# A hybrid decoder step on one core: state-space constants made during the matmul groups on another engine, thirteen groups for eleven, and another order of the output projection's first group

## The chip, the core and the metric

The kernel runs on one core of a Trainium2 chip. The metric is device time in microseconds (us), the median of several runs. "PE" is the matmul engine and "PEld" its weight loads, "DVE" the vector engine, "ACT" the activation engine, "POOL" GpSimd, and "SP" the queue from which most transfers are issued.

## The reference

One layer on 536 tokens (16 meta, 512 prompt, 8 sample) of width 2048 is computed in float32. Attention and an S5 state-space branch run side by side and are merged.

```
h = rmsnorm(x) @ w_in                         # 2048 x 8704: q, k, v, z_a, u, z_s, g_a, g_s
o = sink_attention(rope(q), rope(k), v)       # window 128, meta tokens, sinks
dt = exp(log_dt); lam_bar = exp(lam * dt)     # 64 groups x 64 states, complex
b_bar = (lam_bar - 1) / lam * b
hs = scan(lam_bar, b_bar u) (+ lam_bar^n h0 for the sample group)
y = gelu(Re(c hs) + d u); y = y * sigmoid(y @ w_glu + b_glu)
out = x + (sigmoid(g_a) * ((o * silu(z_a)) @ w_attn_out)
         + sigmoid(g_s) * ((y * silu(z_s)) @ w_ssm_out)) @ w_out
```

## The kernel before

**Matmuls.** Every float32 operand is split into a rounded part and its rest (`xh`, `xl` for x; `whi`, `wlo` for a weight unit of 128 x 1024), and a product is three matmuls: hi by hi, lo by hi, hi by lo. The tokens lie in two halves c of 268 columns, of which a matmul streams 260. A *block* (`mm`, L1002) is one set of 128 output columns: 16 slices kt x 3 x 2 halves = 96 matmuls. For a weight unit, SP loads `raw`, ACT rounds `whi`, and DVE subtracts for `wlo` (L881 to L883).

**Groups.** Some blocks are taken in pairs as a *group* (`quad`): the 2 x 2 of (even or odd kt) x (half) is multiplied in the seven-product way of Strassen and Winograd, on sums of x that `taus` made (`tt`) and on sums of weight units that DVE makes in place (L940). One product is 8 x 3 = 24 matmuls (L1205), a group 168. Of x itself a group reads three of four quarters, `xs[0..2]`: the quarter (even kt, c = 1) is not read by any group. `keep3` (L1217) copies a bank of products to a `z` tile, so that the bank is free for the next group. The two `z` tiles of a group go to `gD` in DRAM at its end (L1039) and are the next group's two `z` tiles.

**Order.** (1) x is loaded and split while three blocks run; (2) six more blocks; (3) eleven groups, q = 0 to 10 (`NQ`); (4) `ORDER1`, 23 blocks: "x" (gates), "h" (heads: k, v, q), "u" (state-space inputs); (5) 13 x blocks and block 47; (6) 8 blocks of the gated unit; (7) 16 of the state-space output; (8) 16 of the attention output (L1511 and on, which also make the sums `cb` of the merged activations); (9) the output projection, eight groups, the first with `late=True`: products 1 to 3 run their first seven of eight slices, then their eighth, when the last `cb` is there, then the others.

**Planner.** `Background` holds generators in lanes. After each half of a weight unit (24 matmuls) `step(budget)` adds a credit, and generators run until their yielded costs have used it; `yield None` waits for the next step. `ssm_prep` (the constants `lam`, `lamp`, `Fk`, `T6`, `T11`, `car` of the state space, some 190 small DVE instructions of 32 to 704 columns) is added at the start of (4) and drained at the first "u". From then on `ssm_sets` and one `ssm(n)` for each "u" run, and at (5) `attention` is added, which begins when they are done. In attention, PE's scores (L656) read `QT`, which DVE makes (L640) from rows loaded from DRAM (`sw`, `sb`, `rb`).

Of the kernel before, what the change touches and what calls it, by code (L numbers as in the profile page):

```python
# [29 lines left out]
def acc_exp(nc, pool, out, x, n):  # L30

    v = nc.vector
# [20 lines left out]
def cmul(nc, pool, out, a, br, bi, sh, tag):  # L53

    v = nc.vector
    n = int(np.prod(sh))
    pat = {1: "p (r a) -> p r a", 2: "p (r a b) -> p r a b"}[len(sh)]
    kw = dict(zip("ab", sh))
    t1 = pool.tile([P, 2 * n], F32, name=tag + "1").rearrange(pat, r=2, **kw)
    t2 = pool.tile([P, 2 * n], F32, name=tag + "2").rearrange(pat, r=2, **kw)  # L60
    v.tensor_tensor(out=t1, in0=a, in1=bc(br, 1, 2), op=ALU.mult)
    v.tensor_tensor(out=t2, in0=a, in1=bc(bi, 1, 2), op=ALU.mult)
    v.tensor_tensor(out=out[:, 0], in0=t1[:, 0], in1=t2[:, 1], op=ALU.subtract)
    v.tensor_tensor(out=out[:, 1], in0=t1[:, 1], in1=t2[:, 0], op=ALU.add)


def ssm_prep(nc, cst, tmp, psum, dram, R, ident, a_prm, a_h0):

    v = nc.vector
    prm = cst.tile([P, 3, 32], F32, name="prm")  # L70
    nc.sync.dma_start(out=prm, in_=a_prm)
    h0 = tmp.tile([P, 32, 2, 8], F32, name="h0")
    nc.sync.dma_start(out=h0, in_=a_h0)
    are, aim, ldt = prm[:, 0], prm[:, 1], prm[:, 2]
    dt = tmp.tile([P, 32], F32, name="dt")
    acc_exp(nc, tmp, dt, ldt, 32)
# [4 lines left out]
    acc_exp(nc, tmp, rho, x, 32)  # L81
# [34 lines left out]
    lam = cst.tile([P, 2, 32], F32, name="lam")  # L116
    v.tensor_tensor(out=lam, in0=e1, in1=bc(rho, 1, 2), op=ALU.mult)
    R["lam"] = lam
# [14 lines left out]
    cmul(nc, tmp, Fq, g, are, naim, (32,), "c32_")  # L133

    lamp = cst.tile([P, 2, 4, 32], F32, name="lamp")
    v.tensor_copy(out=lamp[:, :, 0], in_=lam)
    for k, (a, b) in enumerate(((lam, 0), (lamp[:, :, 1], 0), (lamp[:, :, 1], 1))):
        cmul(nc, tmp, lamp[:, :, k + 1], a, lamp[:, 0, b], lamp[:, 1, b], (32,), "c32_")
    R["lamp"] = lamp
    Fk = cst.tile([P, 8, 32], F32, name="Fk")  # L140
    fv = Fk.rearrange("p (r k) a -> p r k a", r=2)
    v.tensor_tensor(out=fv[:, :, 0], in0=Fq, in1=bc(m2, 1, 2), op=ALU.mult)
    cmul(nc, tmp, fv[:, :, 1:4], bc(fv[:, :, 0], 2, 3), lamp[:, 0, 0:3], lamp[:, 1, 0:3], (3, 32), "c96_")
    nF = cst.tile([P, 2, 32], F32, name="nF")
# [30 lines left out]
    def powers(tab, z, cnt, tag):  # L175
# [4 lines left out]
        for i in range(3):  # L180
            nz = tmp.tile([P, 2, 32], F32, name=f"{tag}z{i}")
            cmul(nc, tmp, nz, zs[-1], zs[-1][:, 0], zs[-1][:, 1], (32,), "c32_")
            zs.append(nz)
        n = 1
        for zp in zs:
# [3 lines left out]
            cmul(nc, tmp, tab[:, :, :, n:n + m], tab[:, :, :, 0:m],  # L189
# [14 lines left out]
    cmul(nc, tmp, Z, zs[2], zs[1][:, 0], zs[1][:, 1], (32,), "c32_")  # L204
# [25 lines left out]
    yield 2.0  # L230
# [579 lines left out]
BUDGET = 5.8  # L810
BUDGET2, BUDGET3, BUDGET4 = 5.2, 2.8, 4.2
# [52 lines left out]
class Stream:  # L864
# [6 lines left out]
    def tiles(self, i, pool=None):  # L871
        raw = self.pool.tile([P, 8, P], F32, name="raw", bufs=3)
# [27 lines left out]
class Quads:  # L900
# [9 lines left out]
    def __init__(self, tc, nc, w, first, n, pool, more_raw, more_parts):  # L910
        self.tc, self.nc, self.w, self.first, self.n, self.pool = tc, nc, w, first, n, pool
        self.more, self.mr, self.mp = None, more_raw, more_parts
# [43 lines left out]
def trunk(tc, A, O):  # L956
# [31 lines left out]
    xh = xp.tile([P, 16, 2, CH], F32R, name="xh")  # L988
    xl = xp.tile([P, 16, 2, CH], F32R, name="xl")
# [21 lines left out]
    def mm_x(w0, **kw):  # L1011
        return mm(2, lambda k, c: xh[:, k, c, w0:CH], lambda k, c: xl[:, k, c, w0:CH], w0, **kw)
# [29 lines left out]
    with tc.tile_pool(name="xld", bufs=2, side="right") as xld:  # L1042
# [25 lines left out]
        for kt in range(16):  # L1068
# [9 lines left out]
            nc.scalar.activation(out=xh[:, kt], in_=xr, func=AF.Copy, scale=gain[:, kt:kt + 1])  # L1078
# [3 lines left out]
            v.scalar_tensor_tensor(out=xl[:, kt], in0=xr, scalar=gain[:, kt:kt + 1], in1=xh[:, kt].bitcast(F32),  # L1082
                                   op0=ALU.mult, op1=ALU.subtract)
            for (_, wh, wl), ps in zip(w3, ps3):
                for (wt, xo, f, l) in ((wh, xh, kt == 0, False), (wh, xl, False, False), (wl, xh, False, kt == 15)):
                    for c in range(2):
                        nc.tensor.matmul(ps[:, c, 0:260], lhsT=wt[:, kt % 8], rhs=xo[:, kt, c, 8:CH], start=f, stop=l)  # L1087
# [35 lines left out]
    S, sp, Ds = {}, None, {}  # L1123
# [85 lines left out]
    def quad(qs, x, banks, y, done, late=False, step=lambda: None):  # L1209
# [10 lines left out]
        W = [qs.get() for n in range(4)] if late else None  # L1220
        for n, (bank, k) in enumerate(first):
            if n == 3 and W:
                for m in range(3):
                    product(first[m][0], W[m], x[first[m][1]], False, range(7, 8))
                    keep3(m)
            product(bank, W[n] if W else qs.get(), x[k], n < 3, range(7) if n < 3 and W else range(8))
            if n in (0, 2) and not W:
# [9 lines left out]
        product(a, qs.get(), x[1], True)  # L1237
# [59 lines left out]
    def xpart(k, c):  # L1297
        return lambda p, e: (xh, xl)[e][:, 2 * p + k, c, 8:CH]

    xs = [xpart(0, 0), xpart(1, 0), xpart(1, 1)] + [lambda p, e, n=n: tt[p][:, e, n] for n in range(4)]  # L1300
    for q in range(NQ):
        y = [ev.tile([P, 2, 260], F32, name="z") for n in range(2)]
# [5 lines left out]
        def step():  # L1308
            nonlocal nst
            nst += 1  # L1310
            if q == NQ - 1:
# [13 lines left out]

    scst = tc.tile_pool(name="scst", bufs=1, side="right")
    sc = scst.__enter__()
    spp = tc.tile_pool(name="spp", bufs=1, side="right")
    bg.add(ssm_prep(nc, sc, spp.__enter__(), aux, dram, S, C["idn"], A["prm"], A["h0"]))
    for n_, (kind, n) in enumerate(ORDER1):  # L1330
        if kind == "x":
            xblock(**({} if n_ else dict(pool=aux, name="aux")))
# [7 lines left out]
        if sp is None:  # L1340
            bg.drain()
            spp.__exit__(None, None, None)
# [10 lines left out]
            for t in (S["H"][:, :, :, 8], *(d[:, :, 0] for d in S["d0"])):  # L1353
                nc.gpsimd.memset(t, 0.0)
            S["bu"] = [aux.tile([P, 512], F32, name=n) for n in ("tr", "wg")] + [S["ax"][:, 0]]
            S["kp"] = S["ax"][:, 1, 0:P]
# [344 lines left out]
```

## Time and profile before

| | |
|---|---|
| median of 3 runs | 1285.49 us (1284.97 to 1285.79) |
| the profiled execution | 1285.47 us, span 1283.7 us |
| mean granted clock of PE | 0.996 |
| PE, DVE, ACT, POOL busy | 99%, 75%, 47%, 9% of the span |

A matmul's record is longer than its turn, since matmuls overlap. So a busy PE only says that PE never stood; the turn of one matmul is read from stretches without a gap, length by count.

### The profile page before, as it was taken

To read this page: it belongs to the slowest core of one execution; us is meant where nothing else is said; L and a number is where in the kernel's file an instruction comes from. 1 tells how busy PE (TensorE), PEld (TensorE's weight loads), DVE (VectorE), ACT (ScalarE), POOL (GpSimd) and SP (SyncE) were. 2 spreads that over 40 slices of the span, in tenths; PEclk is the share of its full clock that TensorE was granted. 3 is DMA by queue.
4 is the path that set the end of the run, shared out by engine and by line. 5 is a ranking of instruction groups with operands and counts; after the bars stand their busy time and mean duration, and the time that the engine had idled before them with its cause. 6 is when DMAs were issued, how large, how long until landed. Compare 5 with 4: busy or idle time off the path is not lost.

```text
span 1283.7 us, 26443 instructions
## 1 busy us (share of the span) xinstructions
PE 1266.4 (99%) x10453; PEld 1240.4 (97%) x10453; DVE 963.6 (75%) x1689; ACT 608.7 (47%) x1300; POOL 114.4 (9%) x231
## 2 busy tenths in 40 slices
PE   9999999999999999999999998999999999999998
PEld 8999999999999999999999998999999999999998
DVE  8586788777697567887778649889986567887775
ACT  8554354444426755445522233486556533344342
POOL 0000000000001222222252021111100000000000
PEclk9999999999999999999999998999999999999999
DMA  8544344333435555554553479767765456545441
GB/s 281 209 156 160 117 141 128 125 120 108 142 115 187 171 149 142 160 149 145 161 129 112 135 223 296 237 203 226 255 229 170 147 181 192 186 150 159 144 143 51
DMA packets 102832, 212.86 MB, mean 166 GB/s; under 512 B 21580, under 2 KB 41988, under 8 KB 102676
## 3 DMA queue, kind: packets, MB, share of 16 engines
q1 hardware_dynamic: 94260, 193.77, 47.3%
q0 software_dynamic: 8448, 17.40, 5.3%
q8 instruction: 82, 1.34, 0.4%
q14 instruction: 42, 0.34, 0.1%
HBM read 178.91 MB, written 33.13 MB: 165 GB/s over the span
## 4 chain that ended last, share of the span: by engine, by line
PE 91%; DMA 5%; ACT 2%; DVE 1%; SPq 1%; issue 0%; ACTq 0%; DVEq 0%
PE mm L1002 53%; PE pr L1205 26%; PE wg L705 2%; DMA gD<-z 1%; PE aux L1205 1%; DMA sw<-rawD 1%; PE aux L1002 1%; PE mm L1087 1%; DMA raw<-in_w 1%; PE aux L656 1%; PE aux L657 1%; PE mm L1456 1%; DMA xr<-in_x 1%; PE wg L436 1%; PE tr L436 1%; ACT whi L941 1%
## 5 line engine op out<-in xcount | busy, mean ns | idle before, releaser
L1002 PE MATMUL mm<-xh,whi 128*128 128x260 f32 (+1 forms) x1312 | 270.7, 288 | 0.0
L1002 PE MATMUL mm<-xl,whi 128*128 128x260 f32 (+1 forms) x1312 | 268.7, 285 | 0.0
L1002 PE MATMUL mm<-xh,wlo 128*128 128x260 f32 (+1 forms) x1312 | 268.0, 285 | 0.0
L882 ACT CAST whi<-raw 128x1024 fp32r<-128x1024 f32 (+3 forms) x144 | 139.2, 975 | 223.7 <-PE mm L1002 104.6
L1002 PEld LDWEIGHTS mm<-xh,whi 128*128 128x128 f32 x1312 | 204.2, 190 | 2.9 <-issue 1.6
L942 DVE TENSOR_TENSOR wlo<-raw,whi 128x1024 fp32r<-128x1024 f32 x133 | 159.8, 1223 | 62.7 <-ACT whi L941 58.6
L1002 PEld LDWEIGHTS mm<-xl,whi 128*128 128x128 f32 x1312 | 205.1, 189 | 1.2 <-issue 1.2
L1002 PEld LDWEIGHTS mm<-xh,wlo 128*128 128x128 f32 x1312 | 203.3, 189 | 1.9 <-issue 1.9
L883 DVE TENSOR_TENSOR wlo<-raw,whi 128x1024 fp32r<-128x1024 f32 (+3 forms) x144 | 162.1, 1131 | 52.6 <-ACT whi L882 50.6
L941 ACT CAST whi<-raw 128x1024 fp32r<-128x1024 f32 x133 | 137.2, 1048 | 133.7 <-PE pr L1205 51.9
L1205 PE MATMUL pr<-cb,whi 128*128 128x260 f32 x848 | 153.4, 283 | 2.7 <-ACT whi L941 2.7
L1205 PEld LDWEIGHTS pr<-cb,whi 128*128 128x128 f32 x848 | 130.9, 189 | 3.3 <-ACT whi L941 3.3
L1002 PE MATMUL mm<-Y,whi 128*128 128x260 f32 x768 | 131.3, 289 | 0.0
L1205 PE MATMUL pr<-tau,whi 128*128 128x260 f32 x672 | 121.2, 283 | 0.0
L1205 PE MATMUL pr<-cb,wlo 128*128 128x260 f32 x424 | 119.0, 283 | 0.0
L1002 PEld LDWEIGHTS mm<-Y,whi 128*128 128x128 f32 x768 | 107.4, 189 | 5.0 <-issue 4.2
L1205 PEld LDWEIGHTS pr<-tau,whi 128*128 128x128 f32 x672 | 103.1, 188 | 0.0
L940 DVE TENSOR_TENSOR raw<-raw 128x1024 f32<-128x1024 f32 x76 | 92.9, 1222 | 1.5
L1205 PE MATMUL pr<-tau,wlo 128*128 128x260 f32 x336 | 93.7, 283 | 0.0
L1002 PE MATMUL mm<-A,whi 128*128 128x260 f32 x512 | 82.1, 283 | 0.0
L1002 PE MATMUL mm<-Y,wlo 128*128 128x260 f32 x384 | 79.8, 287 | 0.0
L1205 PEld LDWEIGHTS pr<-cb,wlo 128*128 128x128 f32 x424 | 79.6, 188 | 0.0
(427 smaller groups left out, 2273.2 us busy)
## 6 DMA issues: line engine op xcount, KB each, us to landing
raw<-in_w SPq DMA_DIRECT2D x202, 512.0 KB, 4.3
gD<-z SPq DMA_DIRECT2D x48, 260.0 KB, 2.8
t<-gD SPq DMA_DIRECT2D x32, 260.0 KB, 2.6
cache<-in_vc POOLq DMA_DIRECT2D x16, 286.0 KB, 4.4
cache<-in_kc POOLq DMA_DIRECT2D x15, 288.0 KB, 5.9
xr<-in_x SPq DMA_DIRECT2D x16, 268.0 KB, 4.8
xg<-in_x SPq DMA_DIRECT2D x8, 536.0 KB, 4.3
sD<-z SPq DMA_DIRECT2D x16, 260.0 KB, 2.3
```

The lines of the kernel that those rows point to most:

```text
L436: nc.tensor.matmul(o[n], lhsT=D["CL"][:, 2 * e + n, i, 1:5], rhs=H[:, 2 * e + n, i, 0:140], start=False, stop=(i == 1))
L656: nc.tensor.matmul(ps[:, e, 0:272], lhsT=q, rhs=KH[:, k0:k0 + 272], start=True, stop=False)
L657: nc.tensor.matmul(ps[:, e, 0:272], lhsT=q, rhs=KL[:, k0:k0 + 272], start=False, stop=True)
L705: nc.tensor.matmul(pv[64 * e:64 * e + 64, 0:256], lhsT=V, rhs=pr[:, e::2], start=(i == 0), stop=(i == len(parts) - 1))
L882: nc.scalar.copy(out=hi, in_=raw)
L883: self.dve = nc.vector.tensor_tensor(out=lo, in0=raw, in1=hi.bitcast(F32), op=ALU.subtract).ins
L940: nc.vector.tensor_tensor(out=o, in0=o, in1=i, op=ALU.add)
L941: nc.scalar.copy(out=hi, in_=t)
L942: nc.vector.tensor_tensor(out=lo, in0=t, in1=hi.bitcast(F32), op=ALU.subtract)
L1002: m = nc.tensor.matmul(ps[:, c, 0:W], lhsT=wt[:, k], rhs=xo(kt, c), start=f, stop=l)
L1087: nc.tensor.matmul(ps[:, c, 0:260], lhsT=wt[:, kt % 8], rhs=xo[:, kt, c, 8:CH], start=f, stop=l)
L1205: m = nc.tensor.matmul(bank, lhsT=wt[:, p], rhs=x(p, e), start=first and f and p == 0, stop=l and p == 7, skip_group_check=not first and l ...
```

## The change

- `NQ` is 13, and `ORDER1` has one "x" instead of three and another order; with that 11 instead of 13 x blocks are left for (5).
- x is stored as three quarters (`xh`, `xl`, 8 x 3 x 268) and a fourth in tiles of its own (`xhq`, `xlq`). After the first blocks the fourth's tiles become work space `flats`. In the last group `again` writes the constants from there to DRAM, loads the quarter's x anew (8 transfers) and splits it again; the constants are read back at the start of (4).
- `ssm_prep` runs in the groups with a credit of 0.4 a product. Its `tensor_tensor`, `tensor_scalar`, `tensor_copy` and `memset` go to POOL, the rest (8 `scalar_tensor_tensor` and a `reciprocal`) stays on DVE. What depends on the sample's state is a generator of its own (`ssm_states`), run from the first "u".
- A group's two output tiles are `z` for even q and `t` for odd q while `nx < 31` (q to 10), and `z` afterwards.
- In the output projection's first group the product with `x[1]` is fourth; the first four products run seven slices each, then the eighth slices. Its weights come from the fourth `raw`, which has a place of its own (`fourth`) and is loaded during the last block of (8).

```diff
+class Mostly:
+    def __init__(self, a, b):
+        self.a, self.b = a, b
+    def __getattr__(self, name):
+        return getattr(self.a if name in ("tensor_tensor", "tensor_scalar", "tensor_copy", "memset") else self.b, name)
...
-def ssm_prep(nc, cst, tmp, psum, dram, R, ident, a_prm, a_h0):
-    v = nc.vector
+def ssm_prep(nc, K, tmp, psum, dram, R, ident, a_prm, later):
+    v = Mostly(nc.gpsimd, nc.vector)
...
+def ssm_states(nc, cst, pool, R, a_h0):
+    v = nc.vector
+    A0, N0 = (cst.tile([P, 32, 2, 8], F32, name=n) for n in ("A0", "N0"))
+    nc.sync.dma_start(out=A0, in_=a_h0)
...
+GBUDGET = 0.4
-NA, NQ = 4, 11
+NA, NQ = 4, 13
-ORDER1 = [(k, 0) for k in "xxxhhuhhuhuhhuhuhhuhuhu"]
+ORDER1 = [(k, 0) for k in "xuhuhuhhuhhuhhuhhuhhu"]
...
+            if k == 3 and self.fourth:
+                pool, bufs = self.fourth, 1
...
+        if r < 7 and self.fourth:
+            s = (0, 1, 2, 5, 3, 4, 6)[s]
...
-    xh = xp.tile([P, 16, 2, CH], F32R, name="xh")
-    xl = xp.tile([P, 16, 2, CH], F32R, name="xl")
+    xh, xl = (xp.tile([P, 8, 3, CH], F32R, name=n) for n in ("xh", "xl"))
+    quarter = {}
+    def quarters():
+        for t, n in ((xh, "xhq"), (xl, "xlq")):
+            quarter[id(t)] = xp.tile([P, 8, CH], F32R, name=n)
+    def xk(t, kt, c, w0):
+        if (kt % 2, c) == (0, 1):
+            return quarter[id(t)][:, kt // 2, w0:CH]
+        return t[:, kt // 2, (0, 1 + c)[kt % 2], w0:CH]
+    def xkeep(kt, src, c):
+        g = gain[:, kt:kt + 1]
...
+        for (h, l), s in zip(dst, src):
+            nc.scalar.activation(out=h, in_=s, func=AF.Copy, scale=g)
+        yield
+        for (h, l), s in zip(dst, src):
+            v.scalar_tensor_tensor(out=l, in0=s, scalar=g, in1=h.bitcast(F32), op0=ALU.mult, op1=ALU.subtract)
+        yield
...
-        W = [qs.get() for n in range(4)] if late else None
+        W = [qs.get() for n in range(4)] if late else []
+        early = [(first[n][0], W[n], x[first[n][1]]) for n in range(3)] + [(a, W[3], x[1])] if late else []
+        for p in early:
+            product(*p, True, range(7))
+        for n, p in enumerate(early):
+            product(*p, False, range(7, 8))
+            if n < 3:
+                keep3(n)
...
+    flats = [xp.tile([P, 8 * CH], F32, name="work", tag=n) for n in ("xhq", "xlq")]
+    bg.add(ssm_prep(nc, kept(flats[0][:, 0:NKEPT]), Places([flats[1], flats[0][:, NKEPT:]], spots()), aux, dram, S, C["idn"],
+                    A["prm"], lambda: tc.issue_after(bg.last)))
+    kD = dram.tile([P, NKEPT], F32, name="kept")
+    def again():
+        nc.sync.dma_start(out=kD, in_=flats[0][:, 0:NKEPT])
+        quarters()
+        raw = [qs.more.tile([P, 8, P], F32, name="raw", bufs=3).rearrange("p k n -> p (k n)") for _ in range(3)]
+        raw = [raw[n // 3][:, CH * (n % 3):CH * (n % 3) + CH] for n in range(8)]
+        for n, r in enumerate(raw):
+            nc.sync.dma_start(out=r, in_=A["x"][:, 2 * n, 1])
+        yield 0.0
+        yield None
+        for n, r in enumerate(raw):
+            list(xkeep(2 * n, r, 1))
+            yield 0.5
     for q in range(NQ):
-        y = [ev.tile([P, 2, 260], F32, name="z") for n in range(2)]
+        if q == NQ - 1:
+            bg.drain()
+        y = [ev.tile([P, 2, 260], F32, name="zt"[q % 2 * (nx < 31)]) for n in range(2)]
...
+            if (q, nst) == (NQ - 1, 3):
+                bg.add(again())
+            bg.step(GBUDGET if q < NQ - 1 else 1.2)
...
-    bg.add(ssm_prep(nc, sc, spp.__enter__(), aux, dram, S, C["idn"], A["prm"], A["h0"]))
+    kt_ = sc.tile([P, NKEPT], F32, name="kept")
+    nc.sync.dma_start(out=kt_, in_=kD)
...
-            bg.drain()
-            spp.__exit__(None, None, None)
...
+            bg.add(ssm_states(nc, sc, sp, S, A["h0"]), lane=1)
             bg.add(ssm_sets(), lane=1)
...
+    qs.fourth = ent(tc.tile_pool(name="fourth", bufs=1))
...
-            qs.load(i - 12)
+            qs.load(i - 11)
```

## Rows read from the trace of the kernel before

**Rows 1.** The page: busy time of each engine with its share of the span and its instructions, and the clock granted to PE in 40 slices (tenths of full speed).

```profile
PE 1266.4 (99%) x10453; PEld 1240.4 (97%) x10453; DVE 963.6 (75%) x1689; ACT 608.7 (47%) x1300; POOL 114.4 (9%) x231
PEclk9999999999999999999999998999999999999999
```

**Rows 2.** The chain that ended last, in order of time (start us, us, what): a long piece of the blocks, one of the groups; a transfer at the start of attention; pieces of the output projection's first group.

```profile
56.67 58.64 PE mm L1002 x486
...
139.28 94.04 PE pr L1205 x783
...
774.55 9.77 DMA sw<-rawD
...
1113.96 2.52 PE aux L1205 x21
1116.49 5.05 PE pr L1205 x42
...
1121.86 1.05 ACT whi L941
...
1130.09 0.94 ACT whi L941
```

**Rows 3.** Busy time by stretch (us from the span's start, then PE, PEld, DVE, ACT, POOL with instructions, granted clock, DMA share, GB/s): the first of eleven stretches that cover the groups and the sum over the eleven; the stretch after the groups; two at the start of attention.

```profile
115.30:135.50 20.20, 20.20 (x171) 20.20 (x170) 17.30 (x17) 9.89 (x14) 0.00 (x0) 1.00 0.35 118
...
sum 222.70, PE 220.23 PEld 219.40 DVE 168.54 ACT 102.37 POOL 0.00; mean PE 20.02 PEld 19.95 DVE 15.32 ACT 9.31 POOL 0.00
...
338.00:396.50 58.50, 58.50 (x484) 58.50 (x483) 50.13 (x220) 15.78 (x20) 0.00 (x0) 1.00 0.40 126
...
787.50:789.60 2.10, 0.00 (x0) 0.00 (x0) 2.07 (x4) 1.56 (x3) 0.55 (x1) 1.00 1.00 357
789.70:796.40 6.70, 6.08 (x28) 6.08 (x29) 6.64 (x11) 2.27 (x4) 0.54 (x1) 0.50 0.97 287
```

**Rows 4.** Waits, who for whom: us in total, times, longest us. The first three are of the groups (115 to 340 us), the fourth of the start of attention (738 to 805 us), the last of the output projection's beginning (1100 to 1150 us).

```profile
ACT whi L941 <- PE pr L1205: 40.9, 24, 4.1
ACT z L1217 <- DMA gD<-z: 37.7, 17, 3.2
...
PE pr L1205 <- ACT z L1217: 2.4, 3, 1.3
...
PE aux L656 <- DVE QT L640: 4.3, 1, 4.3
...
PE pr L1205 <- ACT whi L941: 2.7, 3, 1.3
```

**Rows 5.** DVE in the groups (115 to 338 us) by line: count | busy us, mean ns | idle before. `wlo`, the sums of weights, an output's scaling, and an addition of half that width.

```profile
L942 DVE TENSOR_TENSOR wlo<-raw,whi 128x1024 fp32r<-128x1024 f32 x75 | 90.2, 1223 | 37.4 <-ACT whi L941 36.8
L940 DVE TENSOR_TENSOR raw<-raw 128x1024 f32<-128x1024 f32 x42 | 51.4, 1223 | 0.9
L1032 DVE TENSOR_TENSOR z<-z,R 128x520 f32<-128x520 f32 x20 | 13.9, 697 | 0.4
...
L1239 DVE TENSOR_TENSOR z<-z,pr 128x260 f32<-128x260 f32 x11 | 4.6, 419 | 0.0
```

**Rows 6.** Single lines (min/median/max ns, first and last start us, forms): POOL's only instruction that reads SBUF; two of the constants' instructions on DVE; `wlo` and `keep3` over the whole kernel.

```profile
L651 POOL COPY S<-k_attc x16: 188/232/739, 755.5 to 989.8; 128x4 f32<-128x4 f32 x16
...
L47 DVE TENSOR_TENSOR ex_q<-ex_q,ex_r x14: 180/187/193, 349.6 to 361.2; 128x32 f32<-128x32 f32 x14
...
L61 DVE TENSOR_TENSOR ct<-T,zbz x3: 296/354/422, 386.0 to 390.9; 128x128 f32<-128x128 f32 x1, 128x256 f32<-128x256 f32 x1, 128x192 f32<-128x192 f32 x1
...
L942 DVE TENSOR_TENSOR wlo<-raw,whi x133: 1214/1225/1228, 104.7 to 1266.3; 128x1024 fp32r<-128x1024 f32 x133
...
L1217 ACT ACTIVATE z<-pr x55: 375/387/391, 122.0 to 1267.3; 128x260 f32<-128x260 f32 x55
```

**Rows 7.** In order of time (start us, us), POOL and DVE around one of those POOL copies.

```profile
882.42 0.71 POOL L651 COPY S<-k_attc 128x4 f32<-128x4 f32 x1 [3.80 <-ACT Pn L678]
...
882.39 0.69 DVE L1470 TENSOR_TENSOR z<-t,z 128x520 f32<-128x520 f32 x1
```

**Rows 8.** By line and form (count | busy us, mean ns | idle before): two memsets of POOL; the splitting of x on ACT and DVE in the first 50 us.

```profile
L535 POOL MEMSET pm<- 64x512 f32 x1 | 0.5, 523 | 0.0
L535 POOL MEMSET Vm<- 64x256 f32 x1 | 0.3, 307 | 0.1
...
L1078 ACT ACTIVATE xh<-xr,gain 128x536 fp32r<-128x536 f32 x16 | 11.3, 736 | 1.8 <-DMA xr<-in_x 1.8
...
L1082 DVE SCALAR_TENSOR_TENSOR xl<-xr,gain,xh 128x536 fp32r<-128x536 f32 x16 | 11.9, 772 | 5.2 <-ACT xh L1078 5.2
```

**Rows 9.** Transfers: issuing queue, count, KB each, median us from issue to landing.

```profile
raw<-in_w SPq DMA_DIRECT2D x202, 512.0 KB, 4.3
...
xr<-in_x SPq DMA_DIRECT2D x16, 268.0 KB, 4.8
...
sw<-rawD SPq DMA_DIRECT2D x32, 65.0 KB, 4.6
...
out_s_win_k<-in_wk POOLq DMA_DIRECT2D x1, 1016.0 KB, 9.4
```

More of the change, by code (lines that the diff above doesn't have):

```diff
@@ new lines, with __init__, take, tile @@
+class Places:
+    def __init__(self, flats, spots):
+        self.free, self.spots, self.at = [[f, 0] for f in flats], dict(spots), {}
+    def take(self, n):
+        for f in self.free:
+            if f[1] + n <= f[0].shape[1]:
+                f[1] += n
+                return f[0][:, f[1] - n:f[1]]
+        raise ValueError("no place")
+    def tile(self, shape, dt, name=None):
+        n = int(np.prod(shape[1:]))
+        if name not in self.at:
+            spot = self.spots.get(name)
+            if spot:
+                base, o = spot
+                if base not in self.at:
+                    self.at[base] = self.take(self.spots[base, "size"])
+                self.at[name] = self.at[base][:, o:]
+            else:
+                self.at[name] = self.take(n)
+        t = self.at[name][:, 0:n]
+        return shaped(t if dt == F32 else t.bitcast(dt), shape[1:])
@@ L71, in ssm_prep, with kept @@
+def kept(ap):
+    r, o = {}, 0
+    for nm, sh in KEPT:
+        n = int(np.prod(sh))
+        r[nm] = shaped(ap[:, o:o + n], sh)
+        o += n
+    r["Fre"], r["nFre"], r["nFim"] = r["Fk"][:, 0], r["nF"][:, 0], r["nF"][:, 1]
+    return r
+def ssm_prep(nc, K, tmp, psum, dram, R, ident, a_prm, later):
+    v = Mostly(nc.gpsimd, nc.vector)
+    prm = K["prm"]
     nc.sync.dma_start(out=prm, in_=a_prm)
-    h0 = tmp.tile([P, 32, 2, 8], F32, name="h0")
-    nc.sync.dma_start(out=h0, in_=a_h0)
     are, aim, ldt = prm[:, 0], prm[:, 1], prm[:, 2]
@@ L1077, in trunk @@
                 ws.made = ws.i = first + NB0
-            nc.scalar.activation(out=xh[:, kt], in_=xr, func=AF.Copy, scale=gain[:, kt:kt + 1])
+            kp = xkeep(kt, xr, None)
+            next(kp)
             for j in range(NB0):
@@ L1081, in trunk @@
                     ws.piece(first + j, w3[j], slice(kt % 8, kt % 8 + pieces[kt]))
[L1082 to L1083 removed]
+            next(kp)
             for (_, wh, wl), ps in zip(w3, ps3):
@@ L1217, in keep3 @@
                 nc.scalar.activation(out=kept[n][0], in_=first[n][0], func=AF.Copy, scale=kept[n][1])
-        W = [qs.get() for n in range(4)] if late else None
-        for n, (bank, k) in enumerate(first):
[L1222 to L1227, printed above, removed]
+        W = [qs.get() for n in range(4)] if late else []
[6 more added lines that the diff above has]
+                keep3(n)
+        for n, (bank, k) in enumerate(first):
+            if late and n < 3:
+                continue
+            product(bank, qs.get(), x[k], n < 3)
+            if n in (0, 2):
                 keep3(n)
@@ L1412, in trunk, with part, pieces, in_place @@
     bg.add(attention())
-    def part(t):
-        return lambda k, c: t[:, k, 260 * c:260 * c + 260]
+    def part(ts):
+        return lambda k, c: ts[k][:, 260 * c:260 * c + 260]
+    def pieces(t, n):
+        return [t[:, i] for i in range(n)]
+    def in_place(name, tags):
+        return sum((pieces(xp.tile([P, n, 520], F32R, name=name + t[2:], tag=t), n) for t, n in zip(tags, (12, 4))), [])
     def split(src, hi, lo):
```

162 lines of the change are left out of this document (96 added, 66 removed).

## The prediction

> **What bounds the kernel.** I read the page first: PE is busy for 99% of the span at full clock but for one slice [rows 1]. So the end moves by the number of matmuls and by the moments in which PE stands. The chain then gives a matmul's turn: 486 blocks' matmuls in 58.64 us are 0.1207 us each, 783 of the groups in 94.04 us are 0.1201 us [rows 2]. The stretches and the waits say where PE stands. In the groups it is busy for 220.23 of 222.70 us, and 2.4 us of that gap are three waits for `keep3`, which itself waits 37.7 us in 17 waits for the transfer that empties its `z` tile [rows 3, 4]. At the start of attention one wait of 4.3 us for `QT` stands, at the output projection's beginning three waits of 2.7 us for `whi` [rows 4]. The wait in attention costs more than its length: PE's granted clock is 1.00 before and 0.50 (its 1.2 GHz level) for the 6.7 us after it, in which half the work is lost, 3.35 us [rows 3]. DVE is 76% busy in the groups (168.54 of 222.70) and idle there for 4.9 us per group [rows 3]: it is the next limit, since it makes `wlo` and the sums of weights.
>
> The sum below is made against the profiled execution, 1285.47 us (span 1283.7 and 1.8 around it), which is 0.02 from the median of the three runs. I count 0.2%, 2.6 us, as what can be told from no change.
>
> **Matmuls.** Two more groups take in four blocks: 2 x 2 x 96 = 384 matmuls become 2 x 168 = 336. 48 fewer x 0.1202 [rows 2] = -5.8 us. This is sure, as long as what feeds the groups keeps up. A group has seven `wlo` and four sums on DVE where two blocks have four `wlo`: 7 more x 1.22 us [rows 5] x 2 groups = 17 us of DVE, and 6 more `whi` of ACT. The cover is DVE's idle 4.9 us per group, and weights ahead: ACT waits 40.9 us for PE to free weight tiles [rows 4], so splits are ready before PE wants them. Cost: nothing.
>
> **z and t by turns.** For q to 10 a group no longer writes the tiles that the group before it is still sending. Ten of the old eleven groups could wait, and PE's gap was 2.47 us, about 0.25 each. Groups 11 and 12 still take `z` after `z`: 2 x 0.25 = 0.5 stay. Gain 2.0, bounds 0 and 2.5.
>
> **Output projection's first group.** Before, 63 matmuls (2.52 + 5.05 = 7.6 us) ran ahead of the eighth slices, and then PE waited for `whi` that ACT began at 1121.86 and 1130.09 us, eight and sixteen us into the group [rows 2, 4]: the weight tiles of products 1 and 2 came free only with their eighth slices, and the third sum had to be made first. Now 84 matmuls run first, 84 x 0.12 = 10.1 us. The fourth pair needs no sum and a raw tile loaded ahead, so DVE has two sums of 1.22 us [rows 5] less to do before the last `cb`. What is late next is the tile of the sixth pair, free at about 10.5 us, split in 1.05 + 1.22 us, wanted at 14. I leave 0.5 us of wait: gain 2.2, bounds 0 and 2.7.
>
> **The constants.** After the groups, PE stood for none of the 58.50 us in which DVE made them [rows 3], so taking them from there gains nothing. What they cost in the groups is the open question. Counting the code, 189 instructions go to POOL, with 13,400 columns in all, 71 each on average; nine stay on DVE between them. The planner gives them 67 steps of 24 matmuls, 193 us or 9.6 groups. POOL is idle there [rows 3], so its time is free unless it exceeds 193 us, or holds DVE. A POOL copy of four columns takes 188 ns at best and 739 at worst [rows 6]. The worst kind is one that began with a DVE instruction of two SBUF inputs: 882.42 + 0.71 ends with DVE's 882.39 + 0.69 [rows 7]. So POOL waits for DVE. Whether DVE also waits for POOL the trace doesn't show: `wlo` lasts 1214 to 1228 ns everywhere [rows 6], but only 16 such copies run. The bounds for a POOL instruction of 71 columns: 0.188 plus 71 x 1.05 ns (as on DVE from 32 to 256 columns, 187 to 422 ns [rows 6]) = 0.26 us; or 0.188 plus three times (two reads, one write) a memset's 0.84 ns a column (307 to 523 ns for 256 more [rows 8]) x 71 = 0.37 us. All 189 are 49 to 70 us. POOL itself ends in time: at 739 ns each it would need 140 of 193 us. DVE has 70% of its time in instructions with two SBUF inputs (90.2 + 51.4 + 13.9 of 222.7 us [rows 5]); if only these are held, 34 to 49 us are added, against 9.6 x 4.9 = 47 us of idle time. That lies just under the limit on average, but the planner adds 20 to 29 instructions at once and the nine on DVE stand in its queue until POOL's are done, with `wlo` behind them. So I take 1.5 us, bounds 0 and 23 (70 - 47).
>
> The Trainium skill (SBUF — State Buffer, Who interferes with whom) says that a DVE instruction with two SBUF inputs and a GpSimd instruction that reads SBUF exclude each other, whichever began first, for its whole length. The copy above agrees for one direction; for the other no row here speaks. With its GPSIMD Engine Reference (§3.1, about 2.6 cycles an element at 1.2 GHz) an instruction would be 0.19 + 0.15 = 0.34 us, an estimate; with every one holding DVE the cost would be 64 - 47 = 17 us instead of 1.5.
>
> **The quarter of x.** In the last group, after three products (8.7 us), SP is given 983 KB of constants to write and eight loads of 134 KB, and the tiles of the quarter can be filled only when the write has ended. The nearest rows for the write are 4.3 us (512 KB) and 9.4 us (1016 KB, DRAM to DRAM) [rows 9]; the loads are half of an `xr`, 4.8 us, and overlap it. The first ACT copy and DVE subtraction of 268 columns are 0.39 + 0.42 us [rows 5, 6]. So the first slice stands at 8.7 + 9.4 + 0.8 = 18.9 us at the latest, the group ends at 168 x 0.12 = 20.2, and each further slice comes faster than PE's 12 matmuls per pair of slices, 1.44 us. Hidden by 1.3 us, or by 6.4 with the short write. But ACT and DVE stand in order: whoever waits for the write also holds `whi` and `wlo` behind it. I take 1.0, bounds 0 and 8 (rival 2). The read-back of the constants is one more megabyte on SP's queue before the weights of the first blocks, two units ahead; the cover is a unit's 5.8 us. Nothing.
>
> **Small things.** The split of x has 8 more instructions on ACT and DVE, of half width: 2 x 387 - 736 = 38 ns and 2 x 419 - 772 = 66 ns more a pair [rows 5, 6, 8], 0.3 and 0.5 us over the first 30 us, where transfers are waited for: nothing, at most 0.5. The order in (4): from the first "u" on there were 18 blocks and then 13, now 20 and then 11, 31 both times, with the same credits and the same costs. So attention should begin after as many blocks and meet the same wait; I take no change there. POOL's memsets and `uD` transfers come in the same order behind the first "u".
>
> Sum: -5.8 - 2.0 - 2.2 + 1.5 + 1.0 = -7.5, so 1285.47 - 7.5 = **1278.0 us**.
>
> **Rival 1, slower: POOL holds DVE.** Place: groups 0 to 9. It decides when an average POOL instruction holds DVE for more than 47 / 189 = 0.25 us; below, idle time takes it up. At 0.37 us it is 23 us late instead of 1.5: 1278 + 21.5 = 1299.5. For it: the lower bound is already 0.26 if all hold. Against: a third of DVE's time has no second SBUF input, and weights are ahead. The skill's rule would give 17 us, 1293.5. Chance 0.12; in a quarter of it the loss stays under the gain.
>
> **Rival 2: the quarter comes late.** At the start of attention a transfer took 9.8 us where its kind takes 4.6 [rows 2, 9]. Were the write 5 us later, PE would stand for about 4.5 us with the half clock behind it, 3.35: 1278 + 8 = 1286. Against: the groups' transfers are light, a third of the engines' time [rows 3]. Chance 0.12.
>
> **Rival 3: attention's wait goes away.** It hangs on one late load and on where PE's queue has the scores. Shifted transfers can undo it: 1278 - 4.3 - 3.35 = 1270.4. Chance 0.12; nothing speaks for it but that a queue's luck changes.
>
> **Rival 4: the two rearrangements don't do what they say.** The tiles and the new order leave the waits as they were: 1278 + 4.2 = 1282.2. Chance 0.10.
>
> **Chances.** Forecast, 1274.5 to 1281.5: 0.54. Faster by over 0.2% (under 1282.9): the forecast, rival 3 and most of rival 4, 0.75. Within 0.2%: most of rival 2, some of 1 and 4, 0.14. Slower: the rest of 1 and 2, 0.11. The range from 1270 (rival 3) to 1286 (rival 2) leaves out rival 1 and what lies beyond.
>
> **What would show it.** Right: 48 fewer matmuls of 260 columns, no wait of PE for `keep3` in groups 1 to 10, under 1 us of PE's wait for `whi` in the projection's first group, some 190 POOL instructions between 115 and 320 us of 0.26 to 0.37 us, and `wlo` still ready when PE comes. Wrong: `wlo` longer than 1.228 us and PE waiting for DVE in the groups (rival 1), PE standing at the first block after the groups, with a clock of 0.50 behind it (rival 2), or another wait in attention.

## The result and the profile after

The changed kernel takes 1290.98 us (median of 9 runs, 1287.41 to 1293.93), the kernel before beside it 1285.79 us: a ratio of 1.0041 with a 95% interval of [1.0026, 1.0055]. It is slower by 5 us where 7.5 us less were forecast, outside the range. The profiled execution took 1291.91 us, its span is 1290.1. Line numbers below are those of the changed kernel: `whi` and `wlo` in the groups are L1025 and L1026, the sums L1024, a group's matmuls L1319, `keep3` L1331, the write of `gD` L1153, the constants L47 to L287.

The page answers to [rows 1]: 48 matmuls fewer as forecast, the busy time of PE down by only 3.3 us, POOL up from 114 to 240 us, and an 8 for the clock in the fifth slice (the later 8 stands in [rows 1] as well).

```profile
PE 1263.1 (98%) x10405; PEld 1236.8 (96%) x10405; DVE 966.4 (75%) x1536; ACT 622.6 (48%) x1330; POOL 240.0 (19%) x420
...
PEclk9999899999999999999999998999999999999999
```

The chain, by engine and then by line, shows what the kernel before did not have at all: POOL with 11%, on lines of the constants.

```profile
PE 77%; POOL 11%; issue 6%; DMA 3%; ACT 1%; DVE 1%; SPq 1%; POOLq 0%; ACTq 0%; DVEq 0%
PE mm L1116 46%; PE pr L1319 22%; POOL work L69 2%; PE wg L784 2%; POOL work L71 2%; POOL work L70 1%; DMA raw<-in_w 1%; DMA xr<-in_x 1%; PE aux L1116 1%; POOL work L72 1%; POOL work L57 1%; PE aux L1319 1%; POOL work L56 1%; PE wg L515 1%; PE tr L515 1%
```

The stretches, with the columns of [rows 3], find the place: all thirteen groups, then the two stalls in them, then the start of attention.

```profile
117.20:393.70 276.50, 267.80 (x2179) 266.16 (x2178) 213.20 (x222) 124.60 (x176) 124.62 (x184) 0.98 0.39 130
128.00:134.40 6.40, 6.40 (x55) 6.40 (x55) 0.78 (x3) 0.00 (x0) 5.24 (x18) 1.00 0.26 99
134.40:142.00 7.60, 4.34 (x23) 3.82 (x22) 6.58 (x12) 2.30 (x4) 6.76 (x12) 0.72 0.00 1
...
250.00:258.80 8.80, 5.26 (x45) 5.05 (x43) 2.86 (x3) 2.10 (x3) 0.00 (x0) 0.91 0.99 355
258.80:266.00 7.20, 6.47 (x33) 5.88 (x34) 7.07 (x7) 3.83 (x7) 0.00 (x0) 0.63 0.87 286
793.20:800.00 6.80, 3.25 (x15) 3.25 (x16) 6.70 (x11) 3.32 (x5) 0.55 (x1) 0.50 0.91 255
```

2179 matmuls at the 0.1202 us of [rows 2] are 262 us. The groups took 276.5, so 14.5 us were lost there: PE stood for 8.7 us, and the rest, 5.8 us, is put down to the lower clock behind the stalls (0.72 and 0.63 on average).

**Stall 1, a queue on DVE.** First POOL in order of time, then DVE:

```profile
122.38 1.21 POOL L56 TENSOR_TENSOR work<-work 128x32 f32<-128x32 f32 x1
123.68 1.16 POOL L57 TENSOR_SCALAR work<-work 128x32 f32<-128x32 f32 x1
...
128.82 0.25 POOL L56 TENSOR_TENSOR work<-work 128x32 f32<-128x32 f32 x1
129.16 0.29 POOL L57 TENSOR_SCALAR work<-work 128x32 f32<-128x32 f32 x1
```

```profile
122.26 1.23 DVE L1024 TENSOR_TENSOR raw<-raw 128x1024 f32<-128x1024 f32 x1
123.40 3.62 DVE L1026 TENSOR_TENSOR wlo<-raw,whi 128x1024 fp32r<-128x1024 f32 x3
127.32 1.26 DVE L1026 TENSOR_TENSOR wlo<-raw,whi 128x1024 fp32r<-128x1024 f32 x1 [0.30 <-ACT whi L1025]
134.20 0.20 DVE L51 SCALAR_TENSOR_TENSOR work<-work 128x32 f32<-128x32 f32 x1 [5.62 <-POOL work L50]
134.33 1.21 DVE L1024 TENSOR_TENSOR raw<-raw 128x1024 f32<-128x1024 f32 x1
```

The same POOL instruction of 32 columns lasts 1.2 us while DVE runs a sum of weights or `wlo`, and 0.25 us as soon as DVE stands. A busy DVE alone doesn't do it. Of POOL's 57 `tensor_tensor` of 32 columns in the thirteen groups, the 26 with no DVE instruction of two SBUF inputs beside them took 0.23 to 0.26 us, five of these beside other DVE instructions; the other 31 took 0.88 us on average, up to 1.32.

DVE stands because the next instruction in its queue, one of the eight constants' instructions that stayed on DVE (L51), waits for POOL's L50. Behind it stand the sum of weights (L1024) and on ACT its `whi`; behind these, on ACT and DVE, stand the copy and the addition (L1353, L1354) that free a bank of finished products. For these PE waits (us in total, times, longest us; 125 to 165 us):

```profile
PE pr L1319 <- ACT z L1353: 2.3, 1, 2.3
PE pr L1319 <- DVE t L1354: 1.2, 1, 1.2
PE aux L1319 <- DVE z L1354: 0.9, 1, 0.9
```

The wait of 1.2 us, at 161 us, follows a second wait of DVE for POOL (L185 for L184), which ended at 155 us. It lasted 6.1 us, and most of it did not reach PE.

**Stall 2, a queue on SP.** SP's queue around the write of the constants:

```profile
224.61 0.33 SPq L1153 DMA_DIRECT2D gD<-z  x1
248.74 0.33 SPq L1430 DMA_DIRECT2D kept<-work  x1
249.16 0.38 SPq L1153 DMA_DIRECT2D gD<-z  x1
249.65 3.25 SPq L1006 DMA_DIRECT2D raw<-in_w  x4
```

In the code the write belongs to the last group. In SP's queue it stands between the two writes of the fifth group's outputs, and waits there 23.7 us, through the sixth group, for the last of the constants (L287), with four loads of weights behind it. The waits of 240 to 265 us carry it on to PE:

```profile
ACT whi L1025 <- DVE raw L1024: 14.1, 3, 9.7
DVE raw L1024 <- DMA raw<-in_w: 6.9, 1, 6.9
...
PE pr L1319 <- ACT whi L1025: 3.5, 1, 3.5
```

Outside the groups, attention's wait for `QT`, 4.3 us in [rows 4], was 6.9 us in this execution.

### The profile page after: what moved, and what is told of

Its sections match the earlier page's. It is cut to its first block, busy times and chain, and to the rows that moved or that the text cites. A ratio compares the mean times of both kernels' runs of the same rounds, so it can differ in the third digit from the quotient of the medians.

```text
span 1290.1 us, 26491 instructions
## 1 busy us (share of the span) xinstructions
PE 1263.1 (98%) x10405; PEld 1236.8 (96%) x10405; DVE 966.4 (75%) x1536; ACT 622.6 (48%) x1330; POOL 240.0 (19%) x420
## 4 chain that ended last, share of the span: by engine, by line
PE 77%; POOL 11%; issue 6%; DMA 3%; ACT 1%; DVE 1%; SPq 1%; POOLq 0%; ACTq 0%; DVEq 0%
PE mm L1116 46%; PE pr L1319 22%; POOL work L69 2%; PE wg L784 2%; POOL work L71 2%; POOL work L70 1%; DMA raw<-in_w 1%; DMA xr<-in_x 1%; PE aux L1116 1%; POOL work L72 1%; POOL work L57 1%; PE aux L1319 1%; POOL work L56 1%; PE wg L515 1%; PE tr L515 1%
## 5 line engine op out<-in xcount | busy, mean ns | idle before, releaser
L1025 ACT CAST whi<-raw 128x1024 fp32r<-128x1024 f32 x147 | 151.9, 1048 | 158.9 <-DVE raw L1024 80.9
L1026 DVE TENSOR_TENSOR wlo<-raw,whi 128x1024 fp32r<-128x1024 f32 x147 | 182.9, 1266 | 56.6 <-ACT whi L1025 56.2
L1116 PE MATMUL mm<-xh,whi 128*128 128x260 f32 (+1 forms) x888 | 207.1, 287 | 1.7 <-ACT xr L1174 1.7
L1116 PE MATMUL mm<-xh,wlo 128*128 128x260 f32 (+1 forms) x888 | 205.5, 285 | 0.0
L1116 PE MATMUL mm<-xl,whi 128*128 128x260 f32 (+1 forms) x888 | 204.1, 284 | 0.0
L1319 PE MATMUL pr<-cb,whi 128*128 128x260 f32 x848 | 153.1, 283 | 1.8 <-ACT whi L1025 1.8
L1116 PEld LDWEIGHTS mm<-xh,whi 128*128 128x128 f32 x888 | 147.6, 189 | 5.6 <-issue 2.5
L1319 PE MATMUL pr<-tau,whi 128*128 128x260 f32 x800 | 146.1, 284 | 3.5 <-ACT z L1353 2.3
L1116 PEld LDWEIGHTS mm<-xh,wlo 128*128 128x128 f32 x888 | 147.6, 189 | 1.1 <-issue 1.0
L1116 PEld LDWEIGHTS mm<-xl,whi 128*128 128x128 f32 x888 | 148.0, 189 | 0.0
L1319 PEld LDWEIGHTS pr<-cb,whi 128*128 128x128 f32 x848 | 130.9, 189 | 2.0 <-ACT whi L1025 2.0
L1319 PEld LDWEIGHTS pr<-tau,whi 128*128 128x128 f32 x800 | 123.7, 189 | 3.9 <-ACT z L1353 2.5
L1319 PE MATMUL pr<-cb,wlo 128*128 128x260 f32 x424 | 119.1, 283 | 0.0
L1319 PE MATMUL pr<-tau,wlo 128*128 128x260 f32 x400 | 113.1, 283 | 0.0
L1024 DVE TENSOR_TENSOR raw<-raw 128x1024 f32<-128x1024 f32 x84 | 104.0, 1238 | 8.3 <-DMA raw<-in_w 6.9
L1116 PE MATMUL mm<-Y,whi 128*128 128x260 f32 x576 | 105.9, 288 | 0.3 <-DVE Y L1575 0.3
L1319 PE MATMUL pr<-xh,whi 128*128 128x260 f32 x304 | 85.4, 287 | 3.6 <-ACT whi L1025 3.5
L1319 PE MATMUL pr<-xh,wlo 128*128 128x260 f32 x304 | 86.3, 285 | 0.6 <-DVE wlo L1026 0.6
L1319 PE MATMUL pr<-xl,whi 128*128 128x260 f32 x304 | 86.1, 285 | 0.0
```

Of the source, the lines that this page charges most:

```text
L1024: nc.vector.tensor_tensor(out=o, in0=o, in1=i, op=ALU.add)
L1025: nc.scalar.copy(out=hi, in_=t)
L1026: nc.vector.tensor_tensor(out=lo, in0=t, in1=hi.bitcast(F32), op=ALU.subtract)
L1116: m = nc.tensor.matmul(ps[:, c, 0:W], lhsT=wt[:, k], rhs=xo(kt, c), start=f, stop=l)
L1319: m = nc.tensor.matmul(bank, lhsT=wt[:, p], rhs=x(p, e), start=first and f and p == 0, stop=l and p == 7, skip_group_check=not first and l ...
```

## The experiments

Theory A: POOL is slow because DVE's instructions with two SBUF inputs keep it out; its lateness reaches PE through two queues that run in order, DVE's and SP's. Rival B: POOL's instructions hold DVE, which has no time left for `wlo`. Rival C: other parts of the change cost. The first four runs stood beside a kernel before of 1284.84 us, later ones beside 1285.59 (e5 to e8), 1285.83 (e9, e10) and 1284.73 (e11, e12).

**The constants on DVE** (the changed kernel, one line):

```diff
-    v = Mostly(nc.gpsimd, nc.vector)
+    v = nc.vector
```

> The changed kernel with the constants' instructions on DVE instead of POOL, everything else as changed. Theory A (POOL's constants run late, since DVE's two-input instructions keep them out, and two queues that work in order stand behind them: DVE at its scalar_tensor_tensor near 128 to 134 us, SP at the write of the constants near 225 to 249 us; each makes PE stand 4 to 5 us and lose 3.4 us more at half clock): both stalls go, 1291.0 - 14.6 = about 1276.5 us. Theory B (POOL's instructions hold DVE, whose wlo becomes longer): also about 1276.5, and no wlo over 1.23 us. Theory C (POOL is not the cause: the two more groups or the quarter's way back are): it stays near 1291.

1275.55 us, ratio 0.9926 [0.9908, 0.9944]. In place of a loss of 5 us there is a gain of 9: the other parts of the change gain, and the constants on POOL cost some 15 us. C is out; A and B both expected this. On DVE the instructions of L57 last 0.17 us and those of L69 with 64 columns 0.22; in the changed kernel they are POOL's, and last 0.63 and 0.88 us on average (count | busy us, mean ns | idle before):

```profile
L69 POOL TENSOR_TENSOR work<-work 128x64 f32<-128x64 f32 x17 | 14.8, 875 | 0.2
...
L57 POOL TENSOR_SCALAR work<-work 128x32 f32<-128x32 f32 x14 | 8.8, 629 | 1.2
```

**No DVE instruction behind POOL.** The eight instructions that stayed on DVE are split into two that POOL takes (L51, L52, L173, L175, L185), for example:

```diff
-    v.scalar_tensor_tensor(out=r, in0=k, scalar=-0.693359375, in1=c, op0=ALU.mult, op1=ALU.add)
+    v.tensor_scalar(out=q, in0=k, scalar1=-0.693359375, scalar2=None, op0=ALU.mult)
+    v.tensor_tensor(out=r, in0=q, in1=c, op=ALU.add)
```

> The changed kernel with each of the eight scalar_tensor_tensor of the constants written as a tensor_scalar and a tensor_tensor, both on POOL, so that DVE has no instruction that waits for POOL but the reciprocal. Theory A: the first stall (near 134 to 144 us, and the wait near 155) goes, the second stays: about 1291.0 - 7.7 = 1283. Theory B: eight more POOL instructions hold DVE a little more, nothing is gained: 1291 or above.

1292.02 us, ratio 1.0048 [1.0029, 1.0067]: no gain, against A's size. But the place moved. Stall 1 is gone, and stall 2 has grown. SP waits 33.4 us for POOL (23.7 in the changed kernel), then PE in the groups for 13.3, and the stretch around that stall runs at half clock. The wait of PE and the stretch:

```profile
PE pr L1324 <- ACT whi L1030: 13.3, 1, 13.3
```

```profile
251.00:268.20 17.20, 6.48 (x26) 5.89 (x27) 9.88 (x9) 5.90 (x8) 0.00 (x0) 0.50 0.89 317
```

The two stalls don't add up. Without stall 1 the fifth group ends earlier, and SP is at the write 7.8 us sooner (250.6 - 33.4 = 217.2 us; in the changed kernel 248.7 - 23.7 = 225.0). But POOL makes the last constant no sooner: SP's write starts at 250.6 us in place of 248.7. What PE no longer loses in stall 1 it loses in stall 2. The run alone fits B's number as well, and it needs the next two to be read.

**The write not on SP:**

```diff
-        nc.sync.dma_start(out=kD, in_=flats[0][:, 0:NKEPT])
+        nc.gpsimd.dma_start(out=kD, in_=flats[0][:, 0:NKEPT])
```

> The changed kernel with the write of the constants to DRAM issued from POOL's queue instead of SP's, so that no load of weights stands behind it. Theory A: the second stall (near 249 to 262 us) goes, the first stays: about 1291.0 - 6.9 = 1284. Theory B: DVE's instructions are as long as before, nothing changes: 1291.

1280.46 us, ratio 0.9964 [0.995, 0.9978]: 10 us less than the changed kernel from one queue. In the groups of the profiled execution it is the expected 6.9 us (269.6 us in place of 276.5); what the rest is, the run doesn't show. The loads of weights now follow the writes of `gD` without a break:

```profile
224.12 5.14 SPq L1153 DMA_DIRECT2D gD<-z  x2
229.36 14.97 SPq L1006 DMA_DIRECT2D raw<-in_w  x4
```

Stall 1 is as it was: PE's waits for L1353 and L1354 are 2.3, 1.4 and 0.9 us, in the changed kernel 2.3, 0.9 and 1.2.

**Both edits:**

> Both edits together: POOL makes all constants but the reciprocal, and writes them. Theory A: no queue stands behind POOL any more, both stalls go although POOL is as slow as before: about 1276.5, as with the constants on DVE, and faster than the kernel before by about 9 us. Theory B: DVE is held as before, 1286 or above.

1274.03 us, ratio 0.9908 [0.989, 0.9926], the lowest median of the study, though e1_constants_on_dve lies within its interval. PE waits for nothing in the groups. The stretch of the groups, and then `wlo` over the whole kernel (min/median/max ns):

```profile
120.50:382.80 262.30, 262.24 (x2179) 261.65 (x2178) 213.07 (x214) 124.87 (x176) 144.33 (x201) 1.00 0.41 137
```

```profile
L1031 DVE TENSOR_TENSOR wlo<-raw,whi x147: 1160/1226/2326, 107.3 to 1258.9; 128x1024 fp32r<-128x1024 f32 x147
```

POOL is no faster than in the changed kernel (144.33 us for 201 instructions, 0.72 each; there 124.62 for 184, 0.68 each), and single `wlo` last up to 2.3 us. The last constant is even later than in the changed kernel, at 269 us in place of 249. None of this costs PE anything once nobody queues behind POOL. That decides for A.

**Work on POOL that nobody waits for** (the kernel before, three instructions at each of 70 steps):

```diff
+                    for n in range(3):
+                        if q < 5:
+                            nc.gpsimd.tensor_tensor(out=sink[:, 0:64], in0=xh[:, n, 0, 0:64].bitcast(F32), ...)
+                        else:
+                            nc.gpsimd.memset(sink[:, 0:64], 0.5)
```

> The kernel before with work on POOL that nobody reads or waits for: at each of the first 70 steps of the groups three instructions of 128x64, in groups 1 to 5 products of two tiles in SBUF (105 of them), in groups 6 to 10 memsets (105). Theory A (VectorE's instructions with two inputs keep POOL out): the products last 0.6 to 1.0 us in the mean with single ones above 1.1, the memsets, which read nothing, at most 0.35; wlo on DVE stays at 1.21 to 1.23 us but for a few; PE waits for none of it, and the time is that of before within 0.2% (about 1285). Rival B (POOL holds DVE): wlo grows to 1.4 us or more in the mean in groups 1 to 5, PE waits for it, and the time is at least 5 us longer (1290 or more).

1288.35 us, ratio 1.0023 [1.0011, 1.0035]. The place is not the one intended: nothing in POOL's queue held these instructions, and all ran from 5 to 95 us, beside the splitting of x. The lengths can be read all the same (min/median/max ns, first and last start):

```profile
L1319 POOL MEMSET sinkp<- x105: 151/151/153, 73.1 to 94.9; 128x64 f32 x105
...
L1317 POOL TENSOR_TENSOR sinkp<-xh x105: 313/648/1405, 4.9 to 72.8; 128x64 f32<-128x64 f32 x105
```

The additions of squares on DVE in the same time (5 to 73 us):

```profile
L1054 DVE TENSOR_TENSOR acc<-acc,xsq 128x536 f32<-128x536 f32 x15 | 12.5, 834 | 0.0
```

What reads SBUF lasts from 0.31 to 1.4 us, what only writes always 0.15, although DVE is busy for 18.3 of the 20 us from 75 to 95, and 94 of the 105 memsets ran beside an instruction of two SBUF inputs. And DVE pays too: the additions of L1054 last 834 ns here and 709 before, the splits of x 832 here and 772 before [rows 8]. So B's mechanism exists, at about 0.1 us an instruction. How much of the 2.8 us comes from it is open: the profiled execution also had a longer wait in attention (8.1 us). B's 5 us did not come.

**The output projection's first group alone** (the kernel before with that part of the change):

> The kernel before with only the reordered first group of the output projection. By the step of the prediction: 2.2 us less (1283), one gap of at most 0.5 us there. By the profile of the changed kernel, where one gap of 2.0 us stood in place of three that made 3.5: 1 to 1.5 us less (1284).

1284.08 us, ratio 0.9991 [0.9978, 1.0004]: the expected size, not told apart from nothing. PE's three waits of 2.7 us for `whi` [rows 4] are one of 1.8, as in the changed kernel, where ACT's order shows why:

```profile
1135.61 1.05 ACT L1025 CAST whi<-raw 128x1024 fp32r<-128x1024 f32 x1 [1.21 <-PE pr L1319]
1136.56 0.38 ACT L1331 ACTIVATE z<-pr 128x260 f32<-128x260 f32 x1
1136.84 1.04 ACT L1025 CAST whi<-raw 128x1024 fp32r<-128x1024 f32 x1
```

The `whi` that PE wants is the last of the three: another tile, which PE must free first, and a `keep3` stand ahead of it in ACT's queue.

**z and t by turns alone** (the kernel before):

```diff
-        y = [ev.tile([P, 2, 260], F32, name="z") for n in range(2)]
+        y = [ev.tile([P, 2, 260], F32, name="zt"[q % 2]) for n in range(2)]
```

> The kernel before with only the two names of the group's y tiles in turn, z and t. By the step of the prediction: 2.0 us less (1283.2), and ScalarE's wait of 37.7 us for the write of gD in the groups goes. Rival (the wait was hidden, or PE waits for something else instead): the same time.

1281.63 us, ratio 0.9969 [0.9955, 0.9984]: 4.0 us less, with an interval of 2.1 to 5.8; the forecast 2.0 lies at its edge. The groups have no gap left; in the stretch whose eleven parts gave 220.23 us in [rows 3], PE is now busy throughout:

```profile
115.30:338.00 222.70, 222.70 (x1857) 222.70 (x1856) 169.82 (x173) 103.56 (x143) 0.00 (x0) 1.00 0.38 128
```

**The number of groups and the order of u and h.** Five runs take these two apart, which the change made together. In the first, e4_both has eleven groups and the old order:

```diff
-NA, NQ = 4, 13
+NA, NQ = 4, 11
-ORDER1 = [(k, 0) for k in "xuhuhuhhuhhuhhuhhuhhu"]
+ORDER1 = [(k, 0) for k in "xxxhhuhhuhuhhuhuhhuhuhu"]
```

> The kernel of e4_both with eleven groups and the plain blocks in their old places (48 matmuls more). If the two groups are worth their matmuls and no more: 48 x 0.12 = 5.8 us longer than e4_both, 1279.8. If what they add to ScalarE and VectorE costs part of it: 1 to 4 us longer (1275 to 1278).

1287.91 us, ratio 1.0019 [1.0008, 1.003]: 13.9 us longer than e4_both, where 48 matmuls are 5.8. PE waits for nothing in the groups; the rest is lost later, in several waits of up to 6.1 us. The same with the constants on DVE (e1_constants_on_dve):

> The kernel of e1_constants_on_dve with eleven groups and the plain blocks in their old places. If the eight microseconds that e8_both_and_eleven_groups lost beyond the 48 matmuls come from the groups themselves (two groups less move everything behind them): as long as there, 1287 to 1290. If they come from what POOL does in the groups: 1275.6 + 5.8 = 1281.4.

1290.04 us, ratio 1.0031 [1.0018, 1.0043]. As long without POOL: its work in the groups is not the cause. Twelve groups, and "xx" ahead of the old order:

> The kernel of e4_both with twelve groups and one plain block in its old place (24 matmuls more). If a group is worth its matmuls: 1274.0 + 2.9 = 1276.9. If a group is worth half of the 13.9 us between e4_both and e8_both_and_eleven_groups: 1281. If only luck of the order stands behind the rest: anything from 1277 to 1285.

1292.78 us, ratio 1.0049 [1.0032, 1.0065]. Outside all three expectations: a group more and the time is longer. So the order was suspected. It was changed alone in both directions:

```diff
# e11: eleven groups, the order of the change behind two more x
+ORDER1 = [(k, 0) for k in "xxxuhuhuhhuhhuhhuhhuhhu"]
# e12: thirteen groups, the old order behind one x
+ORDER1 = [(k, 0) for k in "xhhuhhuhuhhuhuhhuhuhu"]
```

> The kernel of e8_both_and_eleven_groups with the u and h units in the order of the changed kernel (two plain blocks more in front). If the old order of u and h made the 8 us beyond the matmuls: e4_both plus 48 matmuls, 1274.0 + 5.8 = 1279.8. If the number of groups made them: as e8_both_and_eleven_groups, 1287.9.

> The kernel of e4_both with thirteen groups and the u and h units in the order of the kernel before (one plain block in front). If the old order costs: 8 us or more longer than e4_both, 1282 or more, since fewer blocks are left beside attention; with the tail of attention uncovered as in e10_both_twelve_groups up to 1290. If the order is worth nothing: 1274.

With eleven groups the new order takes 1284.48 us, ratio 0.999 [0.9977, 1.0004]: 3.4 us less than the old one, half-way between the two expectations. With thirteen groups the old order takes 1292.91 us, ratio 1.0063 [1.0045, 1.0081], 18.9 us more than the new one in e4_both and above what was expected. Now PE stands at the end of attention, for links of attention's own chain. Two of its waits, and the stretch:

```profile
PE wg L772 <- DVE Pm L763: 3.1, 2, 2.0
PE aux L740 <- DVE S L746: 2.2, 3, 1.3
```

```profile
1000.00:1030.00 30.00, 20.71 (x110) 12.57 (x107) 14.64 (x41) 21.90 (x78) 0.38 (x2) 0.77 0.24 80
```

Two groups more leave two blocks fewer between the first "u" and the end of the x blocks, unless the "u" begin earlier. That is what the order does: by the code 31 blocks follow the first "u" in e4_both, 30 in e10_both_twelve_groups, 29 in e12_thirteen_groups_old_order. That PE stands at the end of attention is read from this one execution. And the count is not all: e8_both_and_eleven_groups and e9_on_dve_eleven_groups have 31 such blocks too and take 8 to 9 us more than e4_both and e1_constants_on_dve beyond their 48 matmuls, e11_eleven_groups_new_order has 33 and takes 5 us more. So the runs show that the order matters; why it does is argued only.

## Why the prediction was wrong

**The step that failed is "The constants"**, +1.5 us in the sum. By the changed kernel against e1_constants_on_dve (1.0041 and 0.9926) they cost 15 us, against e4_both (0.9908) 17. The step's own bounds, 0 and 23, held that; the range up to 1286 left it out with rival 1. With 0 in place of 1.5 the sum would have been -9.0; e1_constants_on_dve measured -9.5 [-11.8, -7.2]. That these agree is in part luck: with the sizes that the runs below gave to the other terms the sum would be -11.0.

Three things about the constants were wrong. First, the bounds for a POOL instruction, 0.26 to 0.37 us, are its length when DVE leaves it alone (0.22 to 0.37 us for 32 and 64 columns at 128.8 to 134.5 us). In the groups DVE doesn't: 124.62 us for 184 instructions are 0.68 each. The row that showed it stood in the prediction, 0.71 us for a copy of four columns beside a DVE instruction of two SBUF inputs [rows 7], but it was used only to ask whether POOL ends in time.

Second, "the nine on DVE stand in its queue until POOL's are done, with `wlo` behind them" was named and not worked out. The eight of them are links in one chain of POOL's instructions: each waits for the whole piece of the chain before it, 5.6 and 6.1 us in the two longest cases. Against such a wait the prediction had weights ahead (rival 1). But what PE ran out of was banks for its products, since the copies that free them stand in the same queues: 3.2 us of PE's waiting behind the first case, 1.2 behind the second.

Third, SP's write was looked for (in the step "The quarter of x") where the code has it, in the last group. In SP's queue it stood at the end of the fifth, behind one write of `gD` and ahead of four loads of weights. No row of the kernel before could show that place. But what stands behind an instruction that waits for POOL was asked for DVE, and behind the write for ACT and DVE, never for SP's queue. Taking the write off this queue alone gave back 10 of the 15 to 17 us (e3_kept_not_on_sp).

The price was then raised by the clock: behind each stall it fell to half (1.2 GHz; 0.72 and 0.63 on average over the stretches above), as [rows 3] show for attention.

**Rival 1** had the right engine and the wrong way. POOL does hold DVE a little: `wlo` averages 1371 ns from 117 to 250 us in the changed kernel, 1219 with the constants on DVE. With 1293 in e4_both PE waits for nothing. DVE's idle time pays for it, as the prediction's count had it. The Trainium skill's rule (SBUF — State Buffer, Who interferes with whom) that the two exclude each other is borne out by POOL's 0.25 and 1.2 us, and by memsets, which read nothing, at 0.15. The 17 us worked out from it in the prediction meant DVE's loss, and that did not come about.

**The other terms.**

- *Matmuls*, -5.8: 48 fewer, as forecast. Between e11_eleven_groups_new_order and e4_both, two groups are worth 0.0082 of the time, 10.5 us; in the two profiled executions (1282.18 and 1278.09 us) 4.1. The runs of one kernel spread over 5 to 7 us, so 5.8 lies within, and what may be beyond is open.
- *z and t*, -2.0: -4.0 [-5.8, -2.1] alone. The one profiled execution of before had 2.47 us of gaps there to give back; its other executions may have had more.
- *Output projection*, -2.2: -1.2 [-2.8, +0.5] alone. "Leave 0.5 us of wait" was the error, 1.8 stayed. The order on ACT, not the age of the tile alone, sets it.
- *The quarter of x*, +1.0: nothing for the way back. PE does not wait at the end of the groups, and the longest wait for one of the loads is ACT's of 1.9 us for `raw`. The write that belongs to this step is stall 2. (Rival 2's 4.5 us of standing would be 5 - 1.3 = 3.7 by the step's own numbers.)
- *The order*, 0: no run isolates it as a difference to the kernel before. "Nothing" covered a part without which thirteen groups cost 19 us more. And the reason given, 31 blocks before and after, is not enough: e8_both_and_eleven_groups has 31 as well.
- *Attention's wait*, 0: 4.3 us became 6.9, and was 2.5 to 8.1 in the other runs, and it goes in part with how soon single small transfers land: DVE's wait for that of `sw` just ahead was 1.8 us before, 2.8 in the changed kernel, 4.3 in e5_idle_pool_work. One profiled execution can't tell a change in it from its spread.

**Open:** before with z/t and the late group alone should give some 5 us; e11_eleven_groups_new_order, which has both, the constants early, the quarter's way back and the new order in eleven groups, gives 0.2 to 1.3. Where these 4 us go was not found.

## What to carry to other kernels

Moving small work to a slow engine is free only if nobody stands in a queue behind it: for each of its results look for the first reader on every in-order queue (a compute engine's, and the one that issues the transfers) and at what is behind that reader there. Cost the work by the rows in which the other engine is busy as it will be, not by the shortest ones. And when work is moved between stages, the order of what is left can be worth more than the work saved: here 19 us against 5.8.

## What the hardware showed that was not expected

- A POOL instruction of 32 columns that reads SBUF took 0.25 us alone and 1.2 us beside DVE's instructions with two SBUF inputs. Over all 184 POOL instructions in the groups the average was 0.68 us.
- The exclusion is not symmetric in price: in e5_idle_pool_work a DVE addition of 0.71 us grew by 0.12 us on average, while POOL's instructions doubled, from 0.31 us at best to a median of 0.65.
- Taking away one wait for a late engine can move it to the next queue: stall 2 grew from 3.5 to 13.3 us of PE's waiting when stall 1 was mended alone, since SP came to its write 7.8 us sooner and POOL was no sooner done.
- With the one stall of 13.3 us in e2_no_dve_behind_pool the granted clock was at half (0.50) over 17.2 us, in which PE was busy for 6.48 us.
